# Shifting tiles by 128 bytes and some weights by 96 bytes in a matmul-bound two-block kernel

## The chip, the cores and the metric

The kernel runs on one core of a Trainium2 chip. The metric is the device time of one execution in microseconds (us). Of three runs of the kernel before the median is 2231.85 us (2231.0 to 2233.54).

## The reference

The reference computes two transformer-like blocks of two layers each, one after the other, on 256 tokens of width 1024, in float32. Every layer is a feed-forward part, a mixer and a second feed-forward part, each with a norm, a modulation by a vector `c` and a gated residual. There are eight feed-forward parts in all, and they hold most of the matrix work:

```
def swiglu(h, wi, wo):                    # wi 1024 x 5632, wo 2816 x 1024
    gt, up = jnp.split(h @ wi, 2, axis=-1)
    return (jax.nn.silu(gt) * up) @ wo
# per layer
x = x + 0.5 * (1.0 + mod[:, 0, 2]) * swiglu(pre(x, 0), ffn_wi[l, 0], ffn_wo[l, 0])
x = x + (1.0 + mod[:, 1, 2]) * mixer(pre(x, 1))
x = x + 0.5 * (1.0 + mod[:, 2, 2]) * swiglu(pre(x, 2), ffn_wi[l, 1], ffn_wo[l, 1])
```

The mixers are a gated linear recurrence (hgrn2) and a differential attention in the first block, and a sparse attention merged with a spatial gate in both layers of the second.

## The kernel before, in words

All matrix work with weights goes through TensorE in float32r. A product of two float32 matrices is made of split operands: each operand is rounded to float32r (`hi`), and the rest is kept as `lo`. Three products are added up: hi times hi, hi times lo, lo times hi. The 256 tokens are two tiles T of 128.

Weights come from HBM in chunks of 512 rows by 512 columns. `load_chunk` (L180) takes a chunk in two halves. It loads each half into a tile `raw` by a DMA from SyncE's queue; ScalarE rounds it into a tile `hi` (L197), and VectorE subtracts into a tile `lo` (L198). There are eight slots of `hi` and eight of `lo`, 4096 bytes each on every partition, and `ahead` fills them as fast as they come free, so the loads run ahead of the matmuls. The modulation weights (`araw`, L264) are multiplied on VectorE in between.

Two kinds of matmul loops use these tiles. In a matmul one operand is stationary: a weight load (LDWEIGHTS, the profile's PEld) brings 128 columns of it into the array. The other is moving and streams through.

- **Token-major** (`mm3`, L444 to L456). Stationary are 128 columns of the activations, moving are 512 columns of a weight chunk. Per row block of 128 there are three matmuls of 512 columns, L454 (activation hi, weight hi), L455 (hi, lo) and L456 (lo, hi). The activations are either `hT`, the normed and transposed input of a part, or a phase's own tiles: `aT` in the second half of a feed-forward part, and `y`, `k`/`q` and `oT` in the output projections of the mixers.
- **Feature-major** (`feature_block`, L538 to L552). Here the weights are stationary and `hT` is moving. L550 loads 128 columns of `hi` and streams 512 columns of `hT` (hi and lo of both token tiles); L552 loads 128 columns of `lo` and streams 256. The two alternate, with a weight load for each. All 140 chunks of the first matrices of the eight feed-forward parts that are not run token-major run so: 140 x 4 blocks of features x 4 row blocks = 2240 pairs. In the very first part they are its chunks 8 to 21, in the other seven 4 to 21. The query and key matrices of the differential attention use a similar loop of 256 columns (L611 to L613).

The order of the work is written out: chunks come in a queue, loads and splits are put ahead by priority, and a wait is set wherever a tile is written or read by another engine.

Tiles lie in SBUF one behind the other in the order of their pools: constants, the tiles kept throughout (among them `x` and `hT`), `raw`, `split` (the slots of `hi`, then of `lo`), `tmp`, and then what each phase opens for itself (`aT`, `gf`, `y`, `k`, `oT` and others). Every partition holds them at the same byte address. In the built program the operands of the matmuls stand at these addresses, here also with their remainder by 256:

| tile | address before | by 256 |
|---|---|---|
| `hT` | 13696 | 128 |
| slots of `hi`, `lo` | 75136 + 4096 n, 107904 + 4096 n | 128 |
| `aT` (hi, lo) | 165376, 187904 | 0 |
| `k`, `q` (hgrn2 output) | 173568, 181760 | 0 |
| `oT` (differential attention output) | 189952, 194048 | 0 |
| `y` (second block's mixers) | 209152 to 215296 | 0 |

All offsets within these tiles, from one 128-column block to the next, are whole multiples of 512 bytes, so a tile's remainder is that of each of its blocks.

Of the kernel before, what the change touches and what calls it, by code (L numbers as in the profile page):

```python
# [10 lines left out]
F32R = mybir.dt.float32r  # L11
# [7 lines left out]
P = 128  # L19
D = 1024  # L20
# [11 lines left out]
W_LATER = 15  # L32
FFN_TR, QK_TR, HN_TR, MRG_TR, NSA_TR = 2, 1, 3, 2, 2
W5, XS, SG, RING, GF = 4, 4, 2, 5, 5
WARM = 60

ADA_SPAN = {"first": (11, 6), "ffn": (5, 5), "hgrn": (2, 11), "diff": (3, 6), "nsa": (2, 6), "last": (3, 10)}
# [27 lines left out]
class Chunk:  # L65


    def __init__(self, src, nk, heads=0):
        self.src = src
        self.nk = nk  # L70
        self.heads = heads
        self.parts = None

    def hi(self, k):
        return self.parts[k // 2][0][:, k % 2, :]
# [5 lines left out]
class Net:  # L81
    def __init__(self, ctx, tc, A):
        self.tc = tc
        self.nc = tc.nc
        self.A = A
        self.const = ctx.enter_context(tc.tile_pool(name="const", bufs=1))
        self.keep = ctx.enter_context(tc.tile_pool(name="keep", bufs=1))
        self.rawp = ctx.enter_context(tc.tile_pool(name="raw", bufs=RAWS))
        self.split = ctx.enter_context(tc.tile_pool(name="split", bufs=HALVES))
        self.tmp = ctx.enter_context(tc.tile_pool(name="tmp", bufs=2))  # L90
        self.psm = ctx.enter_context(tc.tile_pool(name="psm", bufs=6, space=PSUM))
        self.pst = ctx.enter_context(tc.tile_pool(name="pst", bufs=2, space=PSUM))
        self.queue = []
        self.next_item = 0
        self.chunks = []
        self.used = [0, 0]
        self.loaded = 0
        self.pend = []
        self.row_stages = []
        self.araws = []  # L100
        self.gates = {}
        self.phase = None
        self.now = 0
        self.setup()
# [75 lines left out]
    def load_chunk(self, it):  # L180
        nc = self.nc
        it.parts = []
        for h in range((it.nk + 1) // 2):
            n = min(2, it.nk - 2 * h)
            w = it.src[-1][1]
            raw = self.raw()
            for c0, c1, src in it.src:
                if it.heads:
                    for g in range(2):
                        r0 = g * 256 + h * P  # L190
                        nc.sync.dma_start(raw[g * 64:(g + 1) * 64], src[r0:r0 + P].rearrange("(i d) n -> d i n", d=64))
                else:
                    nc.sync.dma_start(raw[:, :n, c0:c1], src[h * 256:h * 256 + n * P].rearrange("(k p) n -> p k n", p=P))
            hi = self.split.tile([P, 2, 512], F32R, tag="hi", name="hi")
            lo = self.split.tile([P, 2, 512], F32R, tag="lo", name="lo")
            r = raw[:, :n, :w]
            nc.scalar.activation(hi[:, :n, :w], r, AF.Copy)  # L197
            nc.vector.tensor_sub(lo[:, :n, :w], r, hi[:, :n, :w].bitcast(F32))  # L198
            it.parts.append((hi, lo))
# [110 lines left out]
    def warm(self):  # L310

        ps = self.bank()
        with self.later(1000):
            for _ in range(WARM):
                self.nc.tensor.matmul(ps.rearrange("p (a b) -> p a b", a=4), lhsT=self.ones,
# [1098 lines left out]
def phases(A, which=None):  # L1414
    out = []
    for b in range(2):
        s = "_2" if b else ""
        wi, wo = (A["ffn_wi"], A["ffn_wo"]) if b == 0 else (A["ffn_w_in_2"], A["ffn_w_out_2"])
        for l in range(2):
            out.append((b, l, 0, ("ffn", wi[l, 0], wo[l, 0])))  # L1420
            out.append((b, l, 1, (("hgrn", "diff")[l] if b == 0 else "nsa", l)))
            out.append((b, l, 2, ("ffn", wi[l, 1], wo[l, 1])))
    return out if which is None else [out[i] for i in which]


def build(ctx, tc, A, which=None):
    net = Net(ctx, tc, A)
    nc = tc.nc
    ph = phases(A, which)
    starts = []  # L1430
    net.next_phase = ph[0][:3]

    def diff_prep():
        net.diff_prep(A["b_qk_g"][0], A["b_lam"][0], A["b_subln"][0], 0.8 - 0.6 * math.exp(-0.3))

    def second_half():
        for kind in (1, 0):
            net.ada_first(kind, 1)
        for T in range(2):
            net.scaled(T, 1)  # L1440
            net.pre(T, (1,))
    for i, (b, l, j, spec) in enumerate(ph):
        ada = net.ada_pieces(b, l, j, 2)
        if i + 1 < len(ph):
            b2, l2, j2, _ = ph[i + 1]
            ada += net.ada_pieces(b2, l2, j2, 1) + net.ada_pieces(b2, l2, j2, 0)
        if spec[0] == "ffn":
            cs = net.ffn_chunks(spec[1], spec[2], i == 0)
        elif spec[0] == "hgrn":
            cs = net.hgrn_chunks(A["a_w_in"][0], A["a_w_out"][0])  # L1450
        elif spec[0] == "diff":
            cs = net.diff_chunks(A["b_w_in"][0], A["b_w_out"][0])
        else:
            cs = net.nsa_chunks(A["mix_w_in_2"][l], A["proj_a_2"][l], A["proj_b_2"][l], A["w_out_2"][l])
        starts.append(len(net.chunks))
        done = 0
        for n, spec_ in enumerate(cs):
            if i == 0 and n == 3:
                net.queue.append(("f", second_half))
            if i + 1 < len(ph) and ph[i + 1][3][0] == "diff" and n == len(cs) // 2:  # L1460
                net.queue.append(("f", diff_prep))
            net.add_w(*spec_)
            skip, tail = ADA_SPAN["first" if i == 0 else spec[0] if i + 1 < len(ph) else "last"]
            want = max(0, n + 1 - skip) * len(ada) // (len(cs) - skip - tail)
            while done < min(want, len(ada)):
                net.add_ada(ada[done])
                done += 1
    net.warm()
    net.ada_first(1, 0)
    for T in range(2):  # L1470
        nc.sync.dma_start(net.x[:, T, :], A["x"][0, T * P:(T + 1) * P, :])
        for h in range(2):
            net.norm_half(T, h)
    net.ada_first(0, 0)
    for T in range(2):
        net.scaled(T, 0)
        net.pre(T, (0,))
    net.ahead()
    net.condition("c_2")
    for i, (b, l, j, spec) in enumerate(ph):  # L1480
        last = i + 1 == len(ph)
        net.phase = b, l, j
        net.next_phase = None if last else ph[i + 1][:3]

        def after(T):
            if not last:
                net.pre(T)
            else:
                for h in range(2):
                    o, rstd = net.xs.pop((T, h)), net.ss[T][:, 3:4]  # L1490
                    if h == 0:
                        nc.scalar.activation(o, o, AF.Copy, scale=rstd)
                    else:
                        nc.vector.tensor_scalar(o, o, rstd, None, op0=OP.mult)
                    nc.sync.dma_start(A["out"][0, T * P:(T + 1) * P, h * 512:(h + 1) * 512], o)
        if last:
            nc.sync.dma_start(net.S, A["final_g_2"][None, :].to_broadcast([P, D]))
            net.rows[1] = None
        if spec[0] == "ffn":
            net.ffn(starts[i], after, i == 0)  # L1500
        elif spec[0] == "hgrn":
            net.hgrn(starts[i], A["a_onorm"][0], after)
        elif spec[0] == "diff":
            net.diff(starts[i], after)
        else:
            net.nsa(starts[i], l, after)
# [22 lines left out]
```

## Time and profile before

| what | value |
|---|---|
| median of three runs | 2231.85 us |
| the profiled execution | 2231.27 us, span of its instructions 2229.5 us |
| TensorE (PE) busy | 2188.1 us, 98% |
| VectorE (DVE) busy | 1787.6 us, 80% |
| ScalarE (ACT) busy | 1233.3 us, 55% |
| DMA, mean | 241 GB/s |
| mean granted TensorE clock | 0.998 of full speed |

The span is the time from the first to the last instruction; 1.8 us of the execution lie around it. Matmuls overlap in the profile: one starts while the one before it still drains, so a matmul's duration in a row (some 390 ns for 512 columns) is longer than the time it adds. What it adds is read from the starts: the time from one start to the next.

### The profile page before, as it was taken

The numbers are of one execution on the slowest core, as the hardware profiler recorded it, in microseconds if no ns is written. First come the engines' busy times: TensorE is split into PE (matmuls) and PEld (weight loads), VectorE is DVE, ScalarE is ACT, GpSimd is POOL, SyncE is SP. The second block draws the span as 40 slices with busy tenths as digits, with TensorE's granted clock in tenths as the row PEclk, the third lists the DMA queues.
The fourth block names the chain that finished last, engine by engine and source line by source line (L and its number), as shares of the span: only waits on it lengthen the run. The fifth ranks groups of instructions, "written<-read, shape, count | busy, mean of one in ns | idle before, by whom it ended". The sixth has DMA issues, their size and how long they took to land. (4 is left out here: it accounts for less than half of the span.)

```text
span 2229.5 us, 33181 instructions
## 1 busy us (share of the span) xinstructions
PE 2188.1 (98%) x12152; PEld 1808.4 (81%) x12152; DVE 1787.6 (80%) x2481; ACT 1233.3 (55%) x2184; POOL 118.3 (5%) x164
## 2 busy tenths in 40 slices
PE   9999999999999989999999999999999999999998
PEld 6888887888888767888888787788878887777886
DVE  7888898787878789878868788887877878887664
ACT  3554645564565577564565446456446644655653
POOL 1000101000000131000000000000000001000000
PEclk9999999999999999999999999999999999999999
DMA  9888865777857766867767786676777778845553
GB/s 299 303 300 292 297 218 191 265 243 261 276 185 270 255 227 224 277 216 268 262 221 242 257 291 202 223 253 199 264 258 255 263 241 268 266 153 185 187 172 108
DMA packets 264788, 537.19 MB, mean 241 GB/s; under 512 B 22083, under 2 KB 52619, under 8 KB 264625
## 3 DMA queue, kind: packets, MB, share of 16 engines
q1 hardware_dynamic: 264184, 534.67, 72.1%
q8 instruction: 95, 1.56, 0.3%
q14 instruction: 69, 0.56, 0.1%
q10 hardware_dynamic: 440, 0.40, 0.1%
HBM read 533.95 MB, written 1.05 MB: 240 GB/s over the span
## 5 line engine op out<-in xcount | busy, mean ns | idle before, releaser
L198 DVE TENSOR_TENSOR lo<-raw,hi 128x1024 fp32r<-128x1024 f32 (+1 forms) x704 | 846.8, 1215 | 253.9 <-ACT hi L197 250.1
L197 ACT ACTIVATE hi<-raw 128x1024 fp32r<-128x1024 f32 (+1 forms) x704 | 732.7, 1055 | 524.1 <-PE mm L456 303.0
L550 PE MATMUL mm<-hT,hi 128*128 128x512 f32 x2240 | 793.6, 399 | 0.0
L552 PE MATMUL mm<-hT,lo 128*128 128x256 f32 x2240 | 629.5, 281 | 0.0
L550 PEld LDWEIGHTS mm<-hT,hi 128*128 128x128 f32 x2240 | 421.5, 188 | 103.9
L552 PEld LDWEIGHTS mm<-hT,lo 128*128 128x128 f32 x2240 | 423.8, 189 | 1.0
L454 PE MATMUL mm<-hi,hT 128*128 128x512 f32 (+1 forms) x832 | 331.0, 398 | 1.3 <-ACT hT L384 1.0
L456 PE MATMUL mm<-hi,hT 128*128 128x512 f32 (+1 forms) x832 | 324.8, 391 | 0.9 <-DVE hT L386 0.9
L455 PE MATMUL mm<-lo,hT 128*128 128x512 f32 (+1 forms) x832 | 323.3, 389 | 0.0
L456 PE MATMUL mm<-hi,aT 128*128 128x512 f32 x704 | 278.4, 395 | 0.0
L454 PE MATMUL mm<-hi,aT 128*128 128x512 f32 x704 | 278.2, 395 | 0.0
L455 PE MATMUL mm<-lo,aT 128*128 128x512 f32 x704 | 277.6, 394 | 0.0
L454 PEld LDWEIGHTS mm<-hi,hT 128*128 128x128 f32 x832 | 156.5, 188 | 40.3 <-issue 8.0
L264 DVE SCALAR_TENSOR_TENSOR acc<-araw,c_2s,acc 128x1024 f32<-128x1024 f32 x144 | 184.1, 1278 | 2.8 <-DMA araw<-ada_w 1.9
L456 PEld LDWEIGHTS mm<-hi,hT 128*128 128x128 f32 x832 | 156.5, 188 | 35.0 <-DVE hT L386 2.1
L455 PEld LDWEIGHTS mm<-lo,hT 128*128 128x128 f32 x832 | 156.6, 188 | 29.6 <-issue 0.7
L264 DVE SCALAR_TENSOR_TENSOR acc<-araw,cs,acc 128x1024 f32<-128x1024 f32 x128 | 163.5, 1278 | 10.6 <-DMA araw<-ada_w 9.9
L455 PEld LDWEIGHTS mm<-lo,aT 128*128 128x128 f32 x704 | 132.6, 188 | 30.4
L456 PEld LDWEIGHTS mm<-hi,aT 128*128 128x128 f32 x704 | 132.5, 188 | 30.4
L454 PEld LDWEIGHTS mm<-hi,aT 128*128 128x128 f32 x704 | 132.6, 188 | 30.3
L535 ACT ACTIVATE aT<-uf 128x256 fp32r<-128x256 f32 x140 | 58.2, 416 | 87.0 <-DVE uf L533 87.0
L248 POOL MEMSET acc<- 128x1024 f32 x34 | 32.5, 957 | 1240.2 <-DVE accl L277 713.2
(287 smaller groups left out, 2164.5 us busy)
## 6 DMA issues: line engine op xcount, KB each, us to landing
araw<-ada_w SPq DMA_DIRECT2D x272, 512.0 KB
raw<-ffn_wi SPq DMA_DIRECT2D x160, 512.0 KB
raw<-ffn_w_in SPq DMA_DIRECT2D x160, 512.0 KB
raw<-ffn_wo SPq DMA_DIRECT2D x88, 512.0 KB
raw<-ffn_w_out SPq DMA_DIRECT2D x88, 512.0 KB
raw<-mix_w_in SPq DMA_DIRECT2D x64, 512.0 KB
raw<-a_w_in SPq DMA_DIRECT2D x32, 512.0 KB
raw<-b_w_in SPq DMA_DIRECT2D x24, 512.0 KB
```

The source lines that it names most:

```text
L197: nc.scalar.activation(hi[:, :n, :w], r, AF.Copy)
L198: nc.vector.tensor_sub(lo[:, :n, :w], r, hi[:, :n, :w].bitcast(F32))
L248: nc.gpsimd.memset(st["acc"], 0.0)
L264: self.nc.vector.scalar_tensor_tensor(acc, raw, self.cs[b][:, k:k + 1], acc, op0=OP.mult, op1=OP.add)
L454: nc.tensor.matmul(ps, lhsT=h, rhs=hi, start=start and i == 0, stop=False)
L455: nc.tensor.matmul(ps, lhsT=h, rhs=lo, start=False, stop=False)
L456: nc.tensor.matmul(ps, lhsT=l, rhs=hi, start=False, stop=stop and i == c.nk - 1)
L535: nc.scalar.activation(hi, u, AF.Copy)
L550: nc.tensor.matmul(ps[f], lhsT=c.hi(k)[:, fs], rhs=x, start=kh == 0 and k == 0, stop=False, skip_group_check=True)
L552: nc.tensor.matmul(ps[f][:, 0:256], lhsT=c.lo(k)[:, fs], rhs=x[:, 0:256], start=False, stop=kh == 1 and k == 3, skip_group_check=True)
```

## The change

Three edits, all of them to where tiles lie. A tile `pad` of 128 bytes is put at the start of the pool `tmp`. The slots of `hi` and `lo` get 4352 bytes in place of 4096. And within its slot a half chunk starts 96 bytes (24 elements) later if it belongs to a chunk that runs feature-major in a feed-forward part.

```
+FM_SHIFT = 24
@@ Chunk.__init__
+        self.feature_major = False
@@ Net.__init__
         self.pst = ctx.enter_context(tc.tile_pool(name="pst", bufs=2, space=PSUM))
+        self.t(self.tmp, [P, 32], tag="pad", bufs=1)
@@ load_chunk
-            hi = self.split.tile([P, 2, 512], F32R, tag="hi", name="hi")
-            lo = self.split.tile([P, 2, 512], F32R, tag="lo", name="lo")
+            s = FM_SHIFT if it.feature_major else 0
+            hi, lo = (self.split.tile([P, D + 64], F32R, tag=n, name=n)[:, s:s + D].rearrange("p (a b) -> p a b", a=2)
+                      for n in ("hi", "lo"))
@@ build
-            net.add_w(*spec_)
+            c = net.add_w(*spec_)
+            net.chunks[c].feature_major = spec[0] == "ffn" and (8 if i == 0 else 4) <= n < 22
```

The addresses that follow from it in the built program:

| tile | address after | by 256 | by 512 |
|---|---|---|---|
| `hT` | 13696 | 128 | 384 |
| slots of `hi`, `lo` | 75136 + 4352 n, 109952 + 4352 n | 128 | 384 or 128, in turn |
| a feature-major half chunk in its slot | 96 more | 224 | 480 or 224 |
| `aT` | 169600, 192128 | 128 | 128 |
| `k`, `q` | 177792, 185984 | 128 | 128 |
| `oT` | 194176, 198272 | 128 | 128 |
| `y` | 213376 to 219520 | 128 | 384 |

Everything behind the slots moves by 16 x 256 + 128 = 4224 bytes. `hT` and `raw` stay where they were. No instruction is added, removed or moved: on each engine the built programs have the same instructions in the same order, with the same waits and the same shapes.

## Rows read from the trace of the kernel before

**Rows 1.** The page: the span, busy time by engine, the 40 slices.

```profile
span 2229.5 us, 33181 instructions
PE 2188.1 (98%) x12152; PEld 1808.4 (81%) x12152; DVE 1787.6 (80%) x2481; ACT 1233.3 (55%) x2184; POOL 118.3 (5%) x164
PEclk9999999999999999999999999999999999999999
GB/s 299 303 300 292 297 218 191 265 243 261 276 185 270 255 227 224 277 216 268 262 221 242 257 291 202 223 253 199 264 258 255 263 241 268 266 153 185 187 172 108
```

**Rows 2.** Waits, longest first: PE's longest; then ACT's for PE and DMA.

```profile
PE tr L397 <- DVE xs L378: 7.5, 15, 0.8
PE tr L397 <- ACT hi L197: 5.9, 9, 0.7
...
ACT hi L197 <- PE mm L456: 303.0, 218, 6.2
...
ACT hi L197 <- PE mm L550: 108.6, 86, 2.8
...
ACT hi L197 <- DMA raw<-ffn_wi: 28.3, 26, 4.6
```

**Rows 3.** Groups by line: count, then busy us and mean ns of one.

```profile
L550 PE MATMUL mm<-hT,hi 128*128 128x512 f32 x2240 | 793.6, 399 | 0.0
L552 PE MATMUL mm<-hT,lo 128*128 128x256 f32 x2240 | 629.5, 281 | 0.0
...
L456 PE MATMUL mm<-hi,aT 128*128 128x512 f32 x704 | 278.4, 395 | 0.0
```

**Rows 4.** Line L454 by operand: durations min/median/max in ns, first and last start.

```profile
L454 PE MATMUL mm<-hi,hT x832: 287/389/793, 25.9 to 2056.7; 128*128 128x512 f32 x161, 128*128 128x280 f32 x6
L454 PE MATMUL mm<-hi,aT x704: 388/393/482, 165.8 to 2221.3; 128*128 128x512 f32 x176
L454 PE MATMUL mm<-hi,y x64: 390/395/498, 1342.8 to 2006.8; 128*128 128x512 f32 x64
L454 PE MATMUL mm<-hi,k x16: 388/396/482, 351.4 to 371.1; 128*128 128x512 f32 x16
L454 PE MATMUL mm<-hi,oT x16: 390/396/483, 862.2 to 884.2; 128*128 128x512 f32 x16
```

**Rows 5.** Timeline of PE, token-major with hT: start us, duration us.

```profile
888.99 0.40 PE L456 MATMUL mm<-hi,hT 128*128 128x512 f32 x1
...
891.30 0.39 PE L454 MATMUL mm<-hi,hT 128*128 128x512 f32 x1
...
899.46 0.39 PE L454 MATMUL mm<-hi,hT 128*128 128x512 f32 x1
```

**Rows 6.** Timeline of PE, token-major with aT.

```profile
1025.01 0.39 PE L454 MATMUL mm<-hi,aT 128*128 128x512 f32 x1
...
1029.89 0.39 PE L454 MATMUL mm<-hi,aT 128*128 128x512 f32 x1
```

**Rows 7.** Timeline of PE, token-major with y.

```profile
1996.18 0.39 PE L455 MATMUL mm<-lo,y 128*128 128x512 f32 x1
...
2003.84 0.40 PE L455 MATMUL mm<-lo,y 128*128 128x512 f32 x1
```

**Rows 8.** Timeline of PE, feature-major pairs, as most run.

```profile
1000.25 0.40 PE L550 MATMUL mm<-hT,hi 128*128 128x512 f32 x1
1000.49 0.28 PE L552 MATMUL mm<-hT,lo 128*128 128x256 f32 x1
1000.60 0.40 PE L550 MATMUL mm<-hT,hi 128*128 128x512 f32 x1
1000.84 0.28 PE L552 MATMUL mm<-hT,lo 128*128 128x256 f32 x1
1000.95 0.40 PE L550 MATMUL mm<-hT,hi 128*128 128x512 f32 x1
1001.19 0.28 PE L552 MATMUL mm<-hT,lo 128*128 128x256 f32 x1
1001.31 0.40 PE L550 MATMUL mm<-hT,hi 128*128 128x512 f32 x1
...
1002.37 0.40 PE L550 MATMUL mm<-hT,hi 128*128 128x512 f32 x1
```

**Rows 9.** Timeline of PE, feature-major pairs, one of the other stretches.

```profile
979.04 0.39 PE L550 MATMUL mm<-hT,hi 128*128 128x512 f32 x1
979.27 0.28 PE L552 MATMUL mm<-hT,lo 128*128 128x256 f32 x1
...
984.24 0.39 PE L550 MATMUL mm<-hT,hi 128*128 128x512 f32 x1
```

## The prediction

> **What bounds the kernel now.** I read the page first [rows 1]: PE is busy for 2188.1 of 2229.5 us, in every slice, at the full granted clock. Next the waits [rows 2]: PE's longest wait in total is 7.5 us, while ACT waits 303.0 and 108.6 us for matmuls to free a slot of `hi`. So PE sets the time, and the others wait for it. What is left to ask is how fast PE runs while it waits for nobody. A duration does not tell that, since matmuls overlap; so I took the two loops that make up most of the busy time [rows 3] and read the starts in the timeline.
>
> The reader is to see that equal instructions run at unequal paces:
>
> - Token-major with `hT`: 36 matmuls from 891.30 to 899.46, 226.7 ns each [rows 5].
> - Token-major with `aT`: 21 from 1025.01 to 1029.89, 232.4 ns [rows 6]. With `y`: 33 from 1996.18 to 2003.84, 232.1 ns [rows 7].
> - Feature-major pairs: 6 from 1000.25 to 1002.37, 353.3 ns [rows 8]; but 15 from 979.04 to 984.24 at 346.7 ns [rows 9].
>
> [...] The kind of matmul, the shape and the number format are the same in the first two items. What differs is where the stationary tile lies: `hT` stands at the same remainder by 256 as the moving chunk (128), while `aT`, `y`, `k` and `oT` stand 128 away. All of L454's medians go with that: 389 ns for `hT`, 393 to 396 for the four others [rows 4]. I read this as the weight load of the next matmul and the stream of the running one getting in each other's way, more or less by their relative address. The other differences (which phase, which neighbours) do not sort the rows: `aT` runs beside gates and loads, `y` inside an attention, `k` and `oT` elsewhere, and all four have the slower value.
>
> **The change part by part.** No instruction, wait or DMA is added or moved, so all of it is the pace of PE's rows.
>
> *The shift by 128 bytes.* It brings `aT`, `y`, `k`, `q` and `oT` to remainder 128, that of the chunks and of `hT`. The token-major matmuls with these tiles are three lines with 704 + 64 + 16 + 16 each [rows 4], together 3 x 800 = 2400. Slower bound: they stay at 232.4 ns, 0 us. Faster bound: all take the 226.7 ns of `hT`, 2400 x 5.7 ns = 13.7 us. I take the faster one, as `hT` is the nearest row there is, less the run-in: after an interruption the first ten with `hT` take 231 ns each (888.99 to 891.30 [rows 5]); with some 40 runs of 60, my estimate, that is 40 x 10 x 4.3 ns = 1.7 us. Term: -12.0 us.
>
> *The longer slots.* With 4352 bytes every second slot keeps its distance from `hT` by 256 but moves by 256 within 512. If 512 were what counts, half of the 2400 matmuls with `hT` (three lines of 800 [rows 4]) would change their pace. The rows have the distance +128 (`aT`) and, counted within 512, -128 (`y`), at one pace [rows 6, 7]; that speaks for 256, and I take 0. Otherwise, at the pace of `aT`: 1200 x 5.7 ns = +6.8 us; a gain is not excluded by a row, but the 226.7 ns of `hT` is the best steady pace I have.
>
> *The shift by 96 bytes.* It puts the stationary `hi` and `lo` of the feature-major loop 96 bytes off from the moving `hT`, where they now stand at the same remainder. No row has this distance. The loop itself shows two paces at one address: 353.3 ns, in a pattern that comes back every three pairs (0.35, 0.35, 0.36 us [rows 8]), and 346.7 ns, every pair alike [rows 9]; I count 129 pairs in the second. So the loop falls into one or the other after an interruption. Bounds: each pair as the slowest of the pattern, 0.36 us: 2240 x 6.7 ns = +15 us. Each step as the shortest in the rows, 0.23 us for L550 [rows 9] and 0.11 for L552 [rows 8], 0.34 us: 2240 x 13.3 ns = -30 us. Between them I take 346.7 ns for the 2111 pairs that do not have it yet, since it is a steady pace of these very lines: 2111 x 6.7 ns = 14.1 us, less 1 us for run-in. Term: -13.1 us.
>
> *What is late next.* A faster PE asks for chunks sooner. DMA moves 292 to 303 GB/s in the first five slices and 108 to 291 after [rows 1], and ACT waits 28.3 us in all for `ffn_wi` [rows 2]. One feed-forward part of eight lies in the first five slices; if loads hold it to its present pace, an eighth of both terms, 3 us, is lost. ACT and DVE have 45% and 20% of the span free, and their tiles' shift by a multiple of 32 bytes adds no work, so I put nothing for them.
>
> Sum: 2231.3 - 12.0 - 13.1 = 2206.2 us for the profiled execution. The median lies 0.6 us above that execution; so 2206.8; I say 2207.
>
> [...]
>
> **The rivals.**
>
> - *The feature-major loop keeps its pace.* 96 bytes off, it falls into another pattern that averages what it has now. For it: two paces exist at one address, so the address alone does not decide [rows 8, 9]. Only the first term is left: 2231.9 - 12.0 = about 2220.
> - *It gets under 346.7 ns.* At 0.34 us for each pair: 2231.9 - 12.0 - 30 = 2190. For it: single steps of 0.23 and 0.11 us exist. Against: no run of pairs has both.
> - *Slower.* The 96 bytes push the loop into a pattern in which every pair is the slow one, 0.36 us: +15 - 12 = +3, 2235 us; with the slots' +6.8 as well it would be 2242. It decides from the point where the mean pair is over 353.3 + 12.0/2.24 = 358.7 ns. For it: the distance is new, the present one is 0, and 0 is the good one in the token-major loop [rows 5, 6]. Against: a third of the pairs are slow now, and nothing says that all would be.
> - *Nothing happens.* The pace goes by something other than the distance of the addresses, such as the tile's layout or the phase. Then 2231.9. Against it: four differently laid out tiles share one value [rows 4].
>
> **How the numbers follow.** Forecast 2207 (2200 to 2213 of its own): 0.42. Feature-major pace kept, 2214 to 2224: 0.22. Under it, 2183 to 2199: 0.18. Slower, 2235 to 2242: 0.09. Nothing, 2229 to 2235: 0.09. For two tenths at most outside, the range goes from 2190 (half of the third case is below) to 2224. A measurement of this kernel tells about 0.2%, 4.5 us, from no change. Faster by more than that: 0.42 + 0.22 + 0.18 = 0.82; within: 0.10; slower: 0.08.
>
> **What would show it.** In the profile after, starts of `aT` matmuls 226.7 ns apart in long runs: the first term right; at 232.4: wrong. Starts of L550's successor 346.7 ns apart, all alike: the second right; a pattern of several pairs: not. Token-major with `hT` at two paces by slot: the slots do count. Busy time of ACT, DVE and the bytes moved stay as they are, and PE's waits stay short; should they grow, most in the first five slices, the loads have become the bound. The forecast is wrong altogether if `aT` keeps its 393 ns median.

## The result and the profile after

The changed kernel takes 2205.79 us (median of four runs, 2204.54 to 2207.3) against 2231.43 us (four runs, 2230.53 to 2233.54): a ratio of 0.9887, 95% interval 0.9873 to 0.99. The interval lies below 1, so the change makes the kernel faster, by 1.1%. The forecast was 2207 us.

The head of the page after; rows as in [rows 1]:

```profile
span 2203.4 us, 33181 instructions
PE 2161.0 (98%) x12152; PEld 1803.5 (82%) x12152; DVE 1785.7 (81%) x2481; ACT 1233.0 (56%) x2184; POOL 116.8 (5%) x164
GB/s 295 310 319 298 302 214 193 270 252 262 273 193 276 263 221 226 286 223 279 262 211 252 265 274 208 224 260 196 270 264 256 263 252 272 254 154 182 191 173 114
```

The span is 26.1 us shorter and PE's busy time 27.1 us. DVE and ACT work as long as before, to 2 us. PE is still at 98%: it does the same work at another pace. The line numbers used here are four higher than before (L458 to L460 are the token-major lines, L554 and L556 the feature-major pair).

The same line by operand, minimum/median/maximum duration in ns, after; it answers [rows 4]:

```profile
L458 PE MATMUL mm<-hi,hT x832: 287/389/791, 26.6 to 2034.0; 128*128 128x512 f32 x161, 128*128 128x280 f32 x6
L458 PE MATMUL mm<-hi,aT x704: 389/389/481, 161.3 to 2195.3; 128*128 128x512 f32 x176
L458 PE MATMUL mm<-hi,y x64: 389/393/504, 1324.8 to 1984.0; 128*128 128x512 f32 x64
L458 PE MATMUL mm<-hi,k x16: 389/393/476, 344.9 to 364.4; 128*128 128x512 f32 x16
L458 PE MATMUL mm<-hi,oT x16: 389/393/478, 849.6 to 870.6; 128*128 128x512 f32 x16
```

`aT` went from 393 to `hT`'s 389 ns. `y`, `k` and `oT` run in short groups between other work, and their medians improve by 2 to 3 ns only. Their mean uninterrupted steps from start to start went from 232.5 to 229.2 ns (`y`), 232.6 to 228.8 (`k`), 232.7 to 229.7 (`q`) and 232.7 to 230.8 (`oT`); `y` has the full effect in its long stretch, as the starts show. The timeline of PE after (start us, duration us), first `aT`, then `y`, then `hT`:

```profile
1018.62 0.39 PE L460 MATMUL mm<-hi,aT 128*128 128x512 f32 x1
...
1027.91 0.39 PE L459 MATMUL mm<-lo,aT 128*128 128x512 f32 x1
...
1974.70 0.39 PE L458 MATMUL mm<-hi,y 128*128 128x512 f32 x1
...
1981.28 0.39 PE L460 MATMUL mm<-hi,y 128*128 128x512 f32 x1
...
876.97 0.39 PE L458 MATMUL mm<-hi,hT 128*128 128x512 f32 x1
...
885.80 0.39 PE L458 MATMUL mm<-hi,hT 128*128 128x512 f32 x1
```

Divide by the matmuls between: 41 with `aT` at 226.6 ns (232.4 in [rows 6]), 29 with `y` at 226.9 (232.1 in [rows 7]), 39 with `hT` at 226.4 (226.7 in [rows 5]; a start is given to 10 ns). The three are now equal. The halves of a chunk lie in slots with remainder 384 and 128 by 512 in turn, and all of these runs go through both, as do the feature-major pairs below.

The feature-major pairs after, which answer [rows 8] and [rows 9]:

```profile
984.83 0.39 PE L554 MATMUL mm<-hT,hi 128*128 128x512 f32 x1
985.06 0.28 PE L556 MATMUL mm<-hT,lo 128*128 128x256 f32 x1
985.18 0.39 PE L554 MATMUL mm<-hT,hi 128*128 128x512 f32 x1
...
990.73 0.39 PE L554 MATMUL mm<-hT,hi 128*128 128x512 f32 x1
```

17 pairs in 5.90 us are 347 ns each. All eight feature-major stretches, taken from the starts, have means of 346.7 or 346.8 ns. Before, 129 pairs of 2240 had that pace; now all do once they run.

Added up over the execution from the starts (each matmul is given the time to the next start; a step over 250 or 260 ns holds an interruption or another clock and is counted apart):

| steps | before us | after us | difference |
|---|---|---|---|
| token-major with aT, y, k, q, oT, uninterrupted (2357) | 547.7 | 536.2 | -11.5 |
| the same, interrupted (42) | 19.9 | 20.4 | +0.5 |
| feature-major, uninterrupted (4466; 4472) | 787.7 | 774.9 | -12.8 |
| feature-major, interrupted or at the low clock (14; 8) | 6.8 | 2.5 | -4.3 |
| token-major with hT, all (2496) | 600.1 | 599.4 | -0.7 |
| all other matmuls and their waits (2776) | 258.2 | 260.5 | +2.3 |

So most of the gain, 24.3 of the table's 26.5 us, is in the two places forecast (first and third line). Most of the fourth line is one stretch of the first feed-forward part. Windows before and after there (us; busy us and instructions of PE, PEld, DVE, ACT, POOL; granted clock; DMA share; GB/s):

```profile
147.00:151.00 4.00, 3.66 (x12) 3.14 (x13) 2.56 (x3) 2.14 (x4) 0.96 (x1) 0.57 0.92 276
```

```profile
143.00:147.00 4.00, 3.24 (x19) 2.54 (x18) 3.87 (x5) 3.33 (x5) 0.96 (x1) 1.00 0.90 310
```

The timeline of PE in the window before, with its idle time and what ended it in brackets:

```profile
143.66 0.28 PE L552 MATMUL mm<-hT,lo 128*128 128x256 f32 x1
145.92 0.50 PE L281 MATMUL tr<-acch,ones 128*128 128x512 f32 x1 [1.98 <-ACT acch L276]
147.34 0.80 PE L282 MATMUL tr<-accl,ones 128*128 128x512 f32 x1 [0.93 <-DVE accl L277]
147.93 0.63 PE L550 MATMUL mm<-hT,hi 128*128 128x512 f32 x1
148.36 0.42 PE L552 MATMUL mm<-hT,lo 128*128 128x256 f32 x1
148.57 0.63 PE L550 MATMUL mm<-hT,hi 128*128 128x512 f32 x1
```

Before, PE waited here for the operands of two matmuls of the modulation (L281 and L282) and then ran at a lower clock for most of these 4 us (granted clock 0.57, and 0.50 from 147.5 to 150.5 us): four pairs took 0.64 us each and a fifth 0.41. After, the wait is shorter (1.61 us from the last pair to the next, 4.27 before) and the granted clock stays at 1.00. That is worth 1.2 us for the pairs and 2.7 us for the wait, and nobody forecast it; the last line of the table shows a part of it given back in other waits. It is not shown to come from the change: over a whole execution the mean granted clock was 0.997 to 0.999 in the four runs of the changed kernel and also in sixteen of the kernel before.

### The profile page after: what moved, and what is told of

It reads as the page before. It is cut to its first block, busy times and chain, and to the rows that moved or that the text cites. A ratio compares the mean times of both kernels' runs of the same rounds, so it can differ in the third digit from the quotient of the medians.

```text
span 2203.4 us, 33181 instructions
## 1 busy us (share of the span) xinstructions
PE 2161.0 (98%) x12152; PEld 1803.5 (82%) x12152; DVE 1785.7 (81%) x2481; ACT 1233.0 (56%) x2184; POOL 116.8 (5%) x164
## 5 line engine op out<-in xcount | busy, mean ns | idle before, releaser
L554 PE MATMUL mm<-hT,hi 128*128 128x512 f32 x2240 | 778.7, 392 | 0.0
L556 PE MATMUL mm<-hT,lo 128*128 128x256 f32 x2240 | 626.2, 280 | 0.0
L554 PEld LDWEIGHTS mm<-hT,hi 128*128 128x128 f32 x2240 | 420.5, 188 | 92.5
L556 PEld LDWEIGHTS mm<-hT,lo 128*128 128x128 f32 x2240 | 420.6, 188 | 1.0
L458 PE MATMUL mm<-hi,hT 128*128 128x512 f32 (+1 forms) x832 | 331.2, 398 | 1.9 <-ACT hT L388 1.1
L460 PE MATMUL mm<-hi,hT 128*128 128x512 f32 (+1 forms) x832 | 324.5, 391 | 0.5 <-DVE hT L390 0.5
L460 PE MATMUL mm<-hi,aT 128*128 128x512 f32 x704 | 274.9, 390 | 0.0
L458 PE MATMUL mm<-hi,aT 128*128 128x512 f32 x704 | 274.9, 390 | 0.0
L458 PEld LDWEIGHTS mm<-hi,hT 128*128 128x128 f32 x832 | 156.7, 188 | 40.7 <-issue 7.8
L460 PEld LDWEIGHTS mm<-hi,hT 128*128 128x128 f32 x832 | 156.4, 188 | 34.1 <-DVE hT L390 1.2
L458 PEld LDWEIGHTS mm<-hi,aT 128*128 128x128 f32 x704 | 132.2, 188 | 27.4
L460 PEld LDWEIGHTS mm<-hi,aT 128*128 128x128 f32 x704 | 132.1, 188 | 27.2
```

The lines of the kernel that those rows point to most:

```text
L458: nc.tensor.matmul(ps, lhsT=h, rhs=hi, start=start and i == 0, stop=False)
L460: nc.tensor.matmul(ps, lhsT=l, rhs=hi, start=False, stop=stop and i == c.nk - 1)
L554: nc.tensor.matmul(ps[f], lhsT=c.hi(k)[:, fs], rhs=x, start=kh == 0 and k == 0, stop=False, skip_group_check=True)
L556: nc.tensor.matmul(ps[f][:, 0:256], lhsT=c.lo(k)[:, fs], rhs=x[:, 0:256], start=False, stop=kh == 1 and k == 3, skip_group_check=True)
```

## The experiments

In all of them the paces are read as above, from one start to the next; "pairs" are feature-major, "distance" is the address of the stationary tile less that of the moving one, by 256 bytes.

### Each half alone

The first kernel has only the 128 bytes:

```
-FM_SHIFT = 24
+FM_SHIFT = 0
-            hi, lo = (self.split.tile([P, D + 64], ...
+            hi, lo = (self.split.tile([P, D], ...
```

Expected: 

> Only the 128-byte shift: slots of 4096 bytes and no 96 bytes. Theory of distance (the pace of a matmul goes by the distance by 256 between the stationary block and the moving stream): aT, y, k and oT stand at distance 0, so aT's matmuls start 226.7 to 227.5 ns apart, feature-major pairs stay at 353 ns as before; 2231.4 - 12 = 2219 us (2217 to 2221). Rival, slots (the longer slots, not the shift, made aT faster): aT stays at 232.4 ns and the time at 2231. Rival, one gain for both loops (a faster loop lets the other settle too): pairs also near 347 ns and 2206.

Measured: 2219.13 us (six runs; 2230.34 for sixteen runs of the kernel before), ratio 0.995, interval 0.9934 to 0.9967. Its lines by operand:

```profile
L458 PE MATMUL mm<-hi,aT x704: 387/389/478, 164.4 to 2210.1; 128*128 128x512 f32 x176
L554 PE MATMUL mm<-hT,hi x2240: 387/398/628, 79.8 to 2149.5; 128*128 128x512 f32 x187
```

`aT` has the fast 389 ns with slots of 4096 bytes, L554 keeps its 398 of before. Mean steps: `aT` 227.3 ns, pairs 352.6. Six of the eight parts have 353.2 to 353.3 ns for a pair; the third and fourth have 350.75, since about a hundred of the 283 pairs of each have 346 or 347. So at the distance 0 the loop still has both of its paces.

The second has all but the 128 bytes:

```
-        self.t(self.tmp, [P, 32], tag="pad", bufs=1)
```

Expected: 

> Only the longer slots and the 96 bytes, without the 128-byte tile: aT, y, k and oT stand at distance 128 as before. Theory of distance: pairs at 346.7 ns, aT at 232.4 ns; 2231.4 - 13.5 = 2218 us (2216 to 2220), so that this and the other half add up to the whole change. Rival, slots: aT at 227 ns too, 2206. Rival, no addition (one bound hides the other): clearly under 2216 or over 2220.

Measured: 2220.41 us (five runs), ratio 0.9954, interval 0.9938 to 0.9971. Its line numbers are one lower than those of the changed kernel:

```profile
L457 PE MATMUL mm<-hi,aT x704: 387/393/482, 163.4 to 2212.9; 128*128 128x512 f32 x176
L553 PE MATMUL mm<-hT,hi x2240: 391/392/633, 80.4 to 2150.9; 128*128 128x512 f32 x187
```

Now `aT` stays at 393 and L553 has 392 ns (mean steps 233.1 and 346.75 ns). Each part does its own work and not the other's, and the longer slots do not make `aT` faster. The time is 0.4 us over the range expected: in the steps the uninterrupted pairs gain 13.7 us, but `aT` stands at 233.1 ns against 232.3 before, so that the uninterrupted token-major steps lose 1.4 us (the sweeps below differ as much between two runs at this distance), and the other matmuls and their waits take 4.2 us more.

The two ratios multiply to 0.9904, with intervals of their own of 0.0017 either way each; the whole change has 0.9887. They add up within these intervals.

### Is it the address or the distance?

```
+        self.t(k, [P, 32], tag="pad")
         self.x = self.t(k, [P, 2, D], tag="x")
```

This is the kernel before, with everything from `x` on moved by 128 bytes.

Expected: 

> The kernel before with a tile of 128 bytes ahead of x: hT, raw, the slots and all phases' tiles move by 128 together, so every address changes and no distance between a stationary and a moving tile does. Theory of distance: aT 232.4 ns, pairs 353.3 ns, 2231.4 us (within 3). Rival, the address itself (a tile is read well at remainder 128 by 256 and badly at 0): hT and the chunks now stand at 0 and aT at 128, so the 2400 matmuls with hT go from 227 to 232 ns, +13 us, and the whole is 2231 to 2245, with aT's pace changed.

Measured: 2230.1 us (ten runs), ratio 0.9998, interval 0.9989 to 1.0008.

```profile
L455 PE MATMUL mm<-hi,hT x832: 288/389/796, 27.2 to 2056.9; 128*128 128x512 f32 x161, 128*128 128x280 f32 x6
L455 PE MATMUL mm<-hi,aT x704: 387/393/482, 165.9 to 2221.6; 128*128 128x512 f32 x176
L551 PE MATMUL mm<-hT,hi x2240: 388/398/481, 83.2 to 2159.4; 128*128 128x512 f32 x187
```

`aT` stands at remainder 128 here, as in the changed kernel, and is slow, since the chunks moved along; `hT` and the chunks stand at 0 and are fast together. So a move of all tiles by 128 bytes, the only common move tried, does nothing; the distance does.

### Eight distances in one kernel

Each of the eight feed-forward parts gets its own distance, for its feature-major weights and for its `aT`:

```
+FFNS = [0, 2, 3, 5, 6, 8, 9, 11]
@@ load_chunk
-            s = FM_SHIFT if it.feature_major else 0
+            s = it.shift
@@ ffn, with k the number of the part
+            if 8 * k:
+                self.t(ap, [P, 8 * k], tag="pad2")
@@ build
+                net.chunks[c].shift = 8 * k
```

Expected: 

> The changed kernel, with another distance in each of the eight feed-forward parts: 0, 32, 64, ... 224 bytes, for the feature-major weights against hT and for aT against the chunks alike. One look, read part by part. Theory of distance: the first part (0) has pairs at 353 ns and aT at 226.7, the fourth (96) pairs at 346.7, the fifth (128) aT at 232.4; the others lie between 340 and 361 ns for a pair and 226 and 233 for aT, by distance. Rival, steady or not at all (96 is nothing special: any distance but 0 gives 346.7): all parts but the first at 346.7 ns. Rival, phase (the part of the program decides): pairs or aT paces that do not sort by distance, 347 and 227 in all parts as in the changed kernel. Time: 2206 plus at most 8 x 2 us.

The second sweep has 8 * ((k + 4) % 8) in both places, so that each distance comes in another part.

Expected: 

> The distances of the first sweep in other parts of the program: the eight feed-forward parts have 128, 160, 192, 224, 0, 32, 64, 96 bytes. Theory of distance: the paces go with the distance, not with the part: pairs at 346.7 ns in the fourth part (224) and the eighth (96) and nowhere else, aT at 227 ns in the fifth (0) alone and near 229.5 in the third (192), 233 elsewhere. Rival, part of the program: the second sweep repeats the first one's list by part, pairs at 346.7 in the fourth and the eighth by accident of the order (224 and 96 swap places), but aT at 227 in the first part. Rival, chance after an interruption: paces that repeat neither list. Time 2216 to 2226.

Measured, means of uninterrupted steps in ns (261 of `aT` and 219 to 285 pairs for each):

```
distance       0     32     64     96    128    160    192    224
pairs, 1st   351.8  349.5  353.3  346.7  351.0  350.1  352.8  346.7
pairs, 2nd   353.2  349.5  353.3  346.7  351.1  350.1  352.8  346.8
aT, 1st      227.1  233.3  233.3  234.1  233.1  233.3  229.5  233.3
aT, 2nd      227.4  233.3  233.3  234.3  232.4  233.3  229.5  233.3
```

The two agree to 0.2 ns but at the distances 0 (pairs) and 0 and 128 (`aT`), although the parts are others. One thing these sweeps cannot tell apart: 96 and 224 fell on the fourth and the eighth part both times. The changed kernel, with 346.7 ns in all eight parts, and the last run below, with 353.3 in just these two, settle that the distance decides and not the part. In the second sweep's fourth part (distance 224) the pairs run alike:

```profile
984.61 0.39 PE L556 MATMUL mm<-hT,hi 128*128 128x512 f32 x1
...
988.08 0.39 PE L556 MATMUL mm<-hT,hi 128*128 128x512 f32 x1
```

Ten pairs in 3.47 us are 347 ns each. In the first sweep the fifth part (distance 128) goes in threes, 0.35, 0.35 and 0.35 to 0.36 us:

```profile
1176.72 0.39 PE L556 MATMUL mm<-hT,hi 128*128 128x512 f32 x1
...
1180.93 0.39 PE L556 MATMUL mm<-hT,hi 128*128 128x512 f32 x1
```

Twelve pairs in 4.21 us are 351 ns each. The times were 2221.58 and 2220.71 us, one run each; beside the second sweep and the two runs below the kernel before took 2225.7 us, one run too, so these times support no verdict, and the paces are what counts. The theory of distance holds, though `aT` at 96 (234.1 ns) is slower than the 233 that were expected as the worst. The rival that any distance but 0 does for the pairs falls: 64 is no better than 0. For `aT` only 0 is good, 192 has about half of the gain, and 128, where it stood before, is one of the slow ones.

### The two weight loads apart

Here k is the number of the part from 0, so that the odd parts in the text (first, third and so on) have an even k.

```
-                      for n in ("hi", "lo"))
+                      for n, s in zip(("hi", "lo"), it.shift))
@@ ffn: in front of aT1 always, in front of aT0 in parts 2, 4, 6, 8
+                if k % 2 or s:
+                    self.t(ap, [P, 32], tag=f"pad{s}")
@@ build
+                net.chunks[c].shift = (0, 24) if k % 2 else (24, 0)
```

Expected: 

> The two weight loads of a loop get different distances. Feature-major: parts 1, 3, 5, 7 have hi 96 and lo 0 bytes off hT, parts 2, 4, 6, 8 hi 0 and lo 96. Token-major: parts 1, 3, 5, 7 have aT's hi at distance 0 and its lo at 128, the others the reverse. Theory of distance, every load counts: neither half is enough, pairs at 349 to 354 ns in all parts, and aT between 228 and 232, slower in the even parts, where two of three loads are at 128 (231 to 233), than in the odd ones (228 to 230). Rival, only the load beside the long stream counts (lo, loaded while the 512 columns of L554 run): even parts at 346.7 ns, odd ones at 353. Rival, only the load beside the short stream: the reverse. Time 2216 to 2226.

Measured: pairs in the odd parts (`hi` 96, `lo` 0) 347.4, 346.7, 346.7 and 346.7 ns; in the even ones (`hi` 0, `lo` 96) 351.6, 348.8, 351.6 and 351.6. `aT` in the odd parts (hi at distance 0, lo at 128) 231.4 ns, in the even ones 233.0 to 233.2. 2225.04 us, one run. An odd part's pairs, then an even one's:

```profile
639.88 0.39 PE L557 MATMUL mm<-hT,hi 128*128 128x512 f32 x1
...
643.34 0.39 PE L557 MATMUL mm<-hT,hi 128*128 128x512 f32 x1
```

```profile
439.93 0.40 PE L557 MATMUL mm<-hT,hi 128*128 128x512 f32 x1
...
443.45 0.39 PE L557 MATMUL mm<-hT,hi 128*128 128x512 f32 x1
```

Ten pairs in 3.46 us against ten in 3.52. My expectation that neither half would be enough is wrong for the pairs: shifting `hi` alone is. For `aT` 228 to 230 ns were expected in the odd parts and 231 to 233 in the even ones, and both came out slower, the even ones barely. `hi` is the block that is loaded while the 256 columns of `lo` before it stream (in the trace of the kernel before, the stream of an L552 starts at 1000.13 us and the next load for L550 at 1000.14). That fits the rival of the short stream, though the even parts are better than its 353 ns. For `aT`, sorted by step: where both the running and the next stationary block stand at 0, the step is 227.9 ns, in the other three combinations 232.8 to 233.5. So a good distance of the next block alone is not enough, and the runs do not say which of the two loads it goes by.

### Between the distances

The pairs stand at 16 + 32 k bytes in the parts k = 0 to 7, `aT` at 0 everywhere; `load_chunk` is that of the run before:

```
+                net.chunks[c].shift = (8 * k + 4, 8 * k + 4)
```

Expected: 

> Feature-major distances between those of the sweeps: 16, 48, 80, 112, 144, 176, 208, 240 bytes in the eight parts, aT at distance 0 everywhere. [...] Time 2206 to 2217.

Measured, pairs in ns; `aT` had 227.1 to 227.4 in all parts:

```
distance      16     48     80    112    144    176    208    240
pairs       346.6  346.8  353.1  353.3  349.3  349.3  349.9  353.3
```

2216.44 us, one run. No part's mean is under 346.6. The good distances are not the neighbours of 96 and 224: 80 and 112 are as slow as 0, and 16 and 48 are good. No distance measured here has a faster pair than the changed kernel; 16, 48, 96 and 224 are equal.

## Why the prediction was right

- **What bounds.** Right. PE's share stayed at 98% and its waits short, and what its steps lost the execution lost. One reading on the way was loose. The nines of the clock's row mean 90% or more and not full speed in every slice: the granted clock was 0.57 from 147 to 151 us and from 833 to 837 us.
- **The 128 bytes, -12.0 us.** Right: -11.5 us in the steps, -11.2 us for this half alone. The bound taken, the pace of `hT`, is the one that came; `aT`'s mean of 227.0 to 227.3 ns lies 0.4 to 0.6 above the steady 226.7, which I put down to the run-in. With the tiles of the short groups it is 536.2 - 2357 x 226.67 ns = 2.0 us, where 1.7 were put.
- **The longer slots, 0.** Right: steps with `hT` are 228.7 ns on the first halves of a chunk (remainder 384 by 512) and 227.8 on the second (remainder 128), and the same halves had 228.8 and 227.9 before, when all slots had 384; the half without the 128 bytes left `aT` at 393 ns. For these two, 256 is what counts.
- **The 96 bytes, -13.1 us.** Right: -12.8 us in the uninterrupted steps, with six more of them. By pairs, 2200 x (352.9 - 346.7) = 13.6 us. The choice of the steady pace among bounds of +15 and -30 us rested on the same lines having it elsewhere [rows 9], and 346.7 is what the loop has at every distance that suits it. It was not derived that 96 would be such a distance, and that it is one was luck: of the sixteen distances measured, four give 346.6 to 346.8 and the rest 349 to 353. With 64 or 240 bytes the first rival, about 2220 us, would have come true. That the pace goes by the distance does not hang on that. The expected slower rival, 0.36 us for each pair, came at none.
- **What is late next, nothing.** Right: ACT waits 29.3 us for `ffn_wi` against 28.3 [rows 2], with up to 319 GB/s in the first five slices, and PE lost none of the pace there. The first part's pairs have 346.7 ns like the others. ACT and DVE, with their tiles moved, work 1233.0 and 1785.7 us, no longer than before.
- **Not forecast.** The stretch of the first part with the shorter wait and the granted clock of 1.00, and 2.3 us more in the other matmuls. All lines of the table but the two forecast ones make -2.2 us, beside -24.3 in the two, for which -25.1 were forecast.
- **The chances.** Those given outside the range are half of 0.18, 0.09 and 0.09, together 0.27 and not two tenths at most.

What stays open is why a distance is good. The runs show that it is the distance, that it repeats by 256 bytes in the two cases compared (0 and 256 in the token-major loop, where the two halves of a chunk have 228.7 and 227.8 ns beside 228.8 and 227.9 before; 96 and 96 less 256 in the pairs, as the halves go from slot to slot, with 346.7 or 346.8 ns in every part), and that for the pairs the shift of `hi` alone is enough (346.7 to 347.4 ns). That a weight load and a stream get in each other's way is my reading; no run shows it.

## What to carry to other kernels

When TensorE is busy all the time and waits for nothing, read the time from one start to the next for equal matmuls: if it differs by place, compare the addresses of the stationary and the moving tile. For the token-major float32r matmuls of 512 columns here the two had best stand at the same remainder by 256 bytes, which was worth 2.2% of the mean `aT` step (232.3 to 227.3 ns); the feature-major loop needed another distance, so a loop of another form has to be measured for itself. A sweep of all distances fits into one kernel if each phase gets another one.

## What the runs showed of the hardware

**The least steady paces.** They are 226.67 ns for a matmul of 512 columns, 346.67 ns for a pair of 512 and 256 columns, and 120.0 ns for a matmul of 256 (the loop L611 to L613, where 331 of 384 steps before have just that), each matmul with a weight load of its own. In the traces before and after, no dozen of such steps of 512 columns in a row has a mean under 226.6 ns and no dozen of pairs one under 346.6; in the loop of 256 columns the least mean of a dozen is 119.1 ns before and 118.1 after. The pair's pace is the sum of the two others. From 256 to 512 columns the step grows by 106.67 ns; if it grows evenly, 13.3 ns of each step do not go with the columns, an estimate from 226.67 and 120.0 ns alone.

**Steps that go by the remainder of their start by 6.667 ns.** In the kernel before, I took the starts of the 2227 uninterrupted L550 by their remainder after division by 6.667 ns (with the trace's times corrected by 1.4 parts in a million, the value that fits best). The remainder explains 88% of the variance of the step to L552, over the whole 2.2 ms and across all waits; remainders by 10, 12, 14 or 16 ns explain a fifth or less. A pattern that repeats within a run sorts itself by such a remainder to some degree. But if each of the 17 stretches between longer waits gets a start of its own at random, and the correction is fitted anew, the remainder explains 49% on average and 69% at most in a hundred trials. The table has the remainders where most starts lie (2025 of the 2227):

```
remainder ns     step to L552, median ns    count
1.5 to 2.5       241                        476
2.5 to 3.5       236                        770
4.0 to 4.8       230                         81
4.8 to 6.2       232                        698
```

So in this trace the same step takes 230 to 241 ns by the remainder of its start, and the same remainders go with the same steps across the waits of the program. The pattern of three pairs fits it: 241 + 120, 236 + 113 and 233 + 117 ns are 1060 ns, 159 times 6.667, and the loop comes back to the same remainder. A pace of 346.67 ns is 52 times 6.667, so every pair starts at the same remainder; in the changed kernel 2030 of 2232 L554 start between 2.7 and 4.0 ns, with the same correction. A steady remainder alone does not make a distance good, though: at the distance 64 nearly all pairs take 353 or 354 ns (280 of 283 in the first sweep), and 353.3 is 53 times 6.667. How the distance and the remainder act together, and what stands behind the 6.667 ns, is not shown by any run.
